# A hybrid transformer layer on one core: scale and shift in two halves of the features, with the first key/value products between them

## The chip, the core and the metric

The kernel runs on one core of a Trainium2 chip. The metric is the device time of one launch in microseconds (us). Engines are called by their names: TensorE (PE in the profile, with PEld for its weight loads), VectorE (DVE), ScalarE (ACT), GpSimd (POOL) and SyncE (SP), which issues most of the loads.

## What is computed

One layer of a diffusion backbone over 1024 latent tokens and 256 context tokens of 1024 features: attention and a gated MLP side by side, then a mixture of 16 experts that choose their tokens. The part that matters here is the start, cut from the reference:

```python
sh1, sc1, gt1, sh2, sc2, gt2 = split(silu(c) @ w_mod + b_mod, 6)      # also for c_ctx
h = rmsnorm(x, g_mix) * (1 + sc1) + sh1                               # modulate
k, v = split(h @ w_kv, 2)                                             # keys_values
```

All of it is needed at float32 precision. TensorE's fast format for 4-byte numbers (float32r in the program) keeps fewer bits, so the kernel splits an operand into a rounded high part and a remainder and adds up three products (high·high, high·low, low·high).

## The kernel before, in words

Only the first 80 us are touched. The program is one straight list per engine (`tc.manual_schedule`): every engine runs its instructions in the order in which the Python code emits them, and an engine that waits holds all that stands behind it.

**Rows of scale and shift.** The first 2048 columns of `w_mod` (1024 of shift, 1024 of scale) are loaded as eight blocks n = 0 to 7 of 512 features by 512 columns, 1 MB each (`mod_load`, L238). Two blocks make one column block of 512. `CB` (L236) sets the order: first both halves of scale, then both of shift. For each block `mod_rows(n)` (L241) splits the weights (`split_to`, L146: ScalarE rounds, L147, VectorE subtracts, L148) and TensorE multiplies them with the four columns `c4` (high and low part of silu(c) and of silu(c_ctx)): eight products of 4 x 512 (L255, L256). `mod_columns` (L258) copies the 4 x 512 result out of PSUM (VectorE, L260) and turns it into columns with four small products (L262). When all four column blocks are there, L296 adds the bias and L297 forms the gain `G1`.

**Tokens.** `x_prep` (L160) takes 128 tokens at a time: a sum of squares on ScalarE (L165), a small step on VectorE (L84), a power on GpSimd (L85), and a scaling on VectorE (L168). The square writes a one-column scratch `r` of which there are three.

**Modulation and first products.** `kv_group(g, side, steps)` (L198) does keys and values of four token tiles (g = 0 and 1) or two (g = 2, the context) over the eight feature blocks j of 128. `modulate(g, n, j)` (L182) transposes block j of the tiles on TensorE (L187), applies scale and shift on ScalarE (L191, `h`), rounds it on VectorE (L193) and forms the remainder on VectorE or, for j = 2, 4, 6 of group 0 (`LOW_P`), on GpSimd (L195). It runs two blocks ahead of the products (L219 to L221, twelve of 128 x 256 per block). `side` is other work that is put between the blocks, `steps[j]` pieces of it after block j: in group 0 `x_prep` of token tiles 4 to 7, in groups 1 and 2 that of the context and the splitting of the next weights (ScalarE and GpSimd). The last two blocks of group 0 already modulate the first two blocks of group 1, so these need token tiles 4 to 7 scaled.

**Loads.** SyncE issues in program order; a load into a buffer in use waits at the head of its queue. The key/value weights (2 x 0.5 MB, L286) go into `rkv`, the buffer of block n = 2.

Of the kernel before, what the change touches and what calls it, by code (L numbers as in the profile page):

```python
# [8 lines left out]
F32 = mybir.dt.float32  # L9
# [4 lines left out]
OP = mybir.AluOpType  # L14
# [3 lines left out]
P = 128  # L18
# [6 lines left out]
DJ = D // P  # L25
# [22 lines left out]
def layer(ctx: ExitStack, tc: tile.TileContext, a, out, dbg=None):  # L48
    nc = tc.nc
# [8 lines left out]
    consts = pool("consts")  # L58
# [29 lines left out]
    NV = 32 + 48 + 8 + 8  # L88
    colv = consts.tile([P, NV], F32, name="colv")
    csil = consts.tile([P, DJ, 2], F32, name="csil")  # L90
    c4 = consts.tile([P, DJ, 4], F32R, name="c4")
    modc = consts.tile([P, 16, 2], F32, name="modc")
    modl = consts.tile([P, 32], F32, name="modl")
    B1, B2 = modc[:, 0:8, :], modl[:, 8:16]
    G1 = consts.tile([P, DJ, 2], F32, name="G1")
# [34 lines left out]
    psA = pool("psA", 1, space=PSUM)  # L130
# [4 lines left out]
    vecs = xs.tile([NV, P], F32, name="vecs")  # L135
# [3 lines left out]
    pv = psA.tile([P, 512], F32, name="tp", bufs=3)  # L139
    nc.tensor.transpose(pv[:, :16], vecs[:16], ident[:16, :16])  # L140
    nc.scalar.activation(csil.rearrange("p j i -> p i j"), pv[:, :16].rearrange("p (i j) -> p i j", i=2), AF.Silu)

    nc.vector.tensor_copy(c4[:, :, 0:2], csil)
    nc.vector.tensor_sub(c4[:, :, 2:4], csil, c4[:, :, 0:2].bitcast(F32))

    def split_to(hi, lo, src, eng=None):  # L146
        nc.scalar.copy(hi, src)  # L147
        (eng or nc.vector).tensor_tensor(lo, src, hi.bitcast(F32), op=OP.subtract)  # L148

    XS = {}  # L150
    gm4 = gm_tiles(F32)

    def x_load(kt):

        XS[kt] = gm4[kt // 2 - 2][:, kt % 2 * D:(kt % 2 + 1) * D] if 4 <= kt < 8 else xs.tile(
            [P, D], F32, name="x", bufs=4)
        nc.sync.dma_start(XS[kt], a["x"][kt * P:(kt + 1) * P, :] if kt < NT else
                          a["ctx"][(kt - NT) * P:(kt - NT + 1) * P, :])
# [23 lines left out]
    def modulate(g, n, j):  # L182

        i = 1 if g == 2 else 0
        pt = psA.tile([P, 512], F32, name="tp", bufs=3)[:, :n * P]
        for t in range(n):
            nc.tensor.transpose(pt[:, t * P:(t + 1) * P], XS[g * 4 + t][:, j * P:(j + 1) * P], ident)  # L187
        h = xs.tile([P, 512], F32, name="h", bufs=2)[:, :n * P]
        pv, hv = (w.rearrange("p (t c) -> p t c", t=n) for w in (pt, h))
        parts = [(slice(0, 2), HA[0]), (slice(2, 4), HA[1])] if g == 0 else [(slice(0, n), HH1 if g == 1 else HHC[0])]  # L190
        nc.scalar.activation(h, pt, AF.Identity, scale=G1[:, j, i:i + 1], bias=B1[:, j, i:i + 1])  # L191
        for t, hi in parts:
            nc.vector.tensor_copy(hi[:, :, j, :], hv[:, t])  # L193
        for t, hi in parts:
            (nc.gpsimd if j in LOW_P[g] else nc.vector).tensor_tensor(HL[g][:, t, j, :], hv[:, t], hi[:, :, j, :].bitcast(F32),  # L195
                                                                      op=OP.subtract)

    def kv_group(g, side, steps):  # L198

        n = 2 if g == 2 else 4  # L200
        ps = [psA.tile([P, 512], F32, name="pj", bufs=4) for _ in range(n)]
        if g == 0:
            modulate(g, n, 0)
            modulate(g, n, 1)
            split_to(*wkv2, rkv[:, 2:4, :])
        for j in range(DJ):
            if j + 2 < DJ:
                modulate(g, n, j + 2)
            elif g < 2:

                if g == 1 and j + 2 == DJ:
                    gmc = [w.rearrange("p (t j c) -> p t j c", t=2, j=DJ) for w in gm_tiles(F32R)]
                    HHC.append(gmc[0])
                    HL.append(gmc[1])
                modulate(g + 1, 4 if g == 0 else 2, j + 2 - DJ)
            for t in range(n):
                hh = (HHC[0][:, t] if g == 2 else h_part(0, g * 4 + t))[:, j, :]
                hl = HL[g][:, t, j, :]
                nc.tensor.matmul(ps[t][:, :256], hh, wkv[j // 4][0][:, j % 4, :], start=(j == 0), stop=False)  # L219
                nc.tensor.matmul(ps[t][:, :256], hh, wkv[j // 4][1][:, j % 4, :], start=False, stop=False)  # L220
                nc.tensor.matmul(ps[t][:, :256], hl, wkv[j // 4][0][:, j % 4, :], start=False, stop=(j == DJ - 1))  # L221
# [9 lines left out]
    wraw = [rawp.tile([P, 4, 512], F32, name="raw") for _ in range(2)]  # L231
# [1 line left out]
        w = w.rearrange("p t j c -> p (t j c)").rearrange("p (n a b) -> p n a b", n=2, a=4)  # L233
        wraw += [w[:, 0], w[:, 1]]
    wraw += [rawp.tile([P, 4, 512], F32, name="raw") for _ in range(2)]
    CB = (2, 3, 0, 1)  # L236

    def mod_load(n):  # L238
        nc.sync.dma_start(wraw[n], rows(a["w_mod"], n % 2 * 512, 512, CB[n // 2] * 512, 512))

    def mod_rows(n):  # L241
        jh = n % 2
        if jh == 0:
            XS["pr"] = psA.tile([P, 512], F32, name="pj", bufs=4)
        pr = XS["pr"]
        pair = w_pair()
        if n < 7:
            for h in range(2):
                split_to(*pair[h], wraw[n][:, h * 2:h * 2 + 2, :])
        for jj in range(4):  # L250
            j = jh * 4 + jj
            wh, wl = w_part(pair, jj)
            if n == 7:
                split_to(wh, wl, wraw[n][:, jj, :])
            nc.tensor.matmul(pr[:4, :], c4[:, j, :], wh, start=(j == 0), stop=False)  # L255
# [12 lines left out]
    for n in range(2, 8):  # L268
        mod_load(n)
    for kt in range(4):  # L270
        x_load(kt)
    pr = None
    for n in range(8):
        mod_rows(n)
        if n == 2:
            pv = psA.tile([P, 512], F32, name="tp", bufs=3)
            nc.tensor.transpose(pv[:, :NV], vecs, ident[:NV, :NV])
            nc.vector.tensor_copy(colv, pv[:, :NV])
            gmixc, gffnc, bmodc, bsc, gfc = (colv[:, i:j] for i, j in ((16, 24), (24, 32), (32, 80), (80, 88), (88, 96)))
        if n % 2 == 0 and n:  # L280
            mod_columns(n // 2 - 1, pr)
        pr = XS["pr"]
        if n == 3:
            rkv = wraw[2]
            for h in range(2):
                nc.sync.dma_start(rkv[:, h * 2:h * 2 + 2, :].rearrange("p a b -> p (a b)").rearrange(  # L286
                    "p (j c) -> p j c", j=4), rows(a["w_in"], h * 512, 512, 512, 256))
            for kt in range(4, 8):
                x_load(kt)
    wkv = w_pair()  # L290
    xst = x_steps(range(4))
    next(xst)
    mod_columns(3, pr)
    for _ in range(2):
        next(xst)
    nc.vector.tensor_tensor(modc, pm1, bmodc[:, :16].unsqueeze(2).to_broadcast([P, 16, 2]), op=OP.add)  # L296
    nc.vector.scalar_tensor_tensor(G1, modc[:, 8:16, :], 1.0, gmixc.unsqueeze(2).to_broadcast([P, DJ, 2]),  # L297
                                   op0=OP.add, op1=OP.mult)
    for _ in xst:
        pass  # L300
    split_to(*wkv[0], rkv[:, 0:2, :])
# [25 lines left out]
    hl1, HH1 = h1_tiles(F32R)  # L327
    HL.append(hl1)
    HHC = []
    kv_group(0, x_steps(range(4, 8)), (1, 1, 2, 2, 2, 1, 1, 1))  # L330
    ws = chain(x_steps((8, 9)), w_steps())
    kv_group(1, ws, (1,) * 8)
    kv_group(2, ws, (1,) * 8)
# [70 lines left out]
    n = 0  # L404
# [1211 lines left out]
```

## Time and profile before

| what | before |
|---|---|
| time, median of 3 runs | 1779.95 us (1779.63 to 1780.12) |
| profiled execution | 1780.84 us, span 1779.1 us |
| TensorE busy | 1708.8 us, 96% of the span |
| VectorE / ScalarE / GpSimd busy | 1591.9 / 1244.1 / 519.9 us |
| the chain that ended last | TensorE 79%, VectorE 14% |

The profile is of one execution. A busy share is an average over very different stages; for a change in one stage the timeline and the chain of waits of that stage are read. TensorE's instructions overlap, so the chain, which gives start-to-start distances, is the better source for the cost of a product than its recorded duration.

### The profile page before, as it was taken

What the parts mean: (1) busy time and instruction counts of PE and PEld (TensorE: products, weight loads), DVE (VectorE), ACT (ScalarE), POOL (GpSimd) and SP (SyncE); (2) the same over time, 40 slices, a digit from 0 to 9 for tenths busy, and PEclk for the clock granted to TensorE, in tenths of its full rate; (3) what the DMA queues carried; (4) which work ended last, traced back from release to release, by engine and by line L of the source; (5) the groups of instructions that cost most, each with busy time, mean ns of one, the idle gap of its engine ahead of it and who ended that gap; (6) DMA issues with size and microseconds to landing.
All of it is one profiled execution on the core that took longest, in us unless ns stands there. A gap on an engine that the chain in (4) does not pass through costs nothing.

```text
span 1779.1 us, 24500 instructions
## 1 busy us (share of the span) xinstructions
PE 1708.8 (96%) x8586; PEld 1405.4 (79%) x8586; DVE 1591.9 (89%) x2371; ACT 1244.1 (70%) x1663; POOL 519.9 (29%) x358
## 2 busy tenths in 40 slices
PE   7999999999999969999999999999999999999997
PEld 4888878778788858777778888888888888888885
DVE  7778777999858999999999999999999999999997
ACT  6632356666653348777777887888878878878886
POOL 1433467787851112423331101101101101101013
PEclk9999999999999979999999999999999999999999
DMA  9357200000025678999999999999999999999994
GB/s 355 102 155 233 84 1 1 18 8 24 13 96 202 236 263 315 346 363 365 360 359 374 392 385 378 390 384 375 389 383 380 386 384 380 385 386 385 378 325 185
DMA packets 204971, 485.69 MB, mean 273 GB/s; under 512 B 10448, under 2 KB 12848, under 8 KB 204848
## 3 DMA queue, kind: packets, MB, share of 16 engines
q1 hardware_dynamic: 200096, 466.83, 70.8%
q0 software_dynamic: 4752, 17.30, 3.8%
q8 instruction: 67, 1.10, 0.3%
q14 instruction: 56, 0.46, 0.1%
HBM read 463.13 MB, written 20.97 MB: 272 GB/s over the span
## 4 chain that ended last, share of the span: by engine, by line
PE 79%; DVE 14%; issue 3%; ACT 2%; DMA 1%; POOL 1%; SPq 0%; POOLq 0%; DVEq 0%; ACTq 0%
PE p L1533 24%; PE p L1536 12%; PE py L1523 6%; PE py L1522 6%; PE py L1524 6%; DVE wlo L148 3%; PE po L768 3%; PE pj L691 2%; PE pj L693 2%; PE pj L692 2%; DVE mx L654 2%; PE tp L1322 2%; DVE ph L753 2%; PE pj L958 2%; PE pj L960 1%
## 5 line engine op out<-in xcount | busy, mean ns | idle before, releaser
L148 DVE TENSOR_TENSOR wlo<-raw,whi 128x1024 fp32r<-128x1024 f32 (+1 forms) x556 | 661.6, 1231 | 46.8 <-ACT whi L147 42.9
L147 ACT CAST whi<-raw 128x1024 fp32r<-128x1024 f32 (+1 forms) x590 | 593.1, 1021 | 118.8 <-PE p L1536 67.1
L755 POOL TENSOR_TENSOR pl<-pf,ph 128x512 fp32r<-128x512 f32 x160 | 218.1, 1385 | 52.3 <-DVE ph L753 19.6
L1533 PE MATMUL p<-whi,xb 128*128 128x512 f32 x512 | 204.9, 400 | 0.0
L1533 PE MATMUL p<-whi,xa 128*128 128x512 f32 x512 | 204.6, 400 | 0.0
L1533 PE MATMUL p<-wlo,xa 128*128 128x512 f32 x512 | 200.0, 391 | 0.3 <-DVE wlo L148 0.2
L1533 PE MATMUL p<-wlo,xb 128*128 128x512 f32 x512 | 199.8, 390 | 0.0
L1523 PE MATMUL py<-wlo,thl 128*128 128x512 f32 x504 | 198.5, 394 | 0.0
L1522 PE MATMUL py<-whi,thl 128*128 128x512 f32 x504 | 197.6, 392 | 0.0
L1524 PE MATMUL py<-whi,thl 128*128 128x512 f32 x504 | 196.3, 389 | 0.0
L1536 PE MATMUL p<-whi,xb 128*128 128x512 f32 x512 | 158.1, 390 | 0.4 <-DVE xb L1485 0.4
L1536 PE MATMUL p<-whi,xa 128*128 128x512 f32 x512 | 158.1, 390 | 0.0
L748 ACT ACTIVATE pf<-st 128x512 f32<-128x512 f32 x160 | 94.9, 598 | 70.3 <-PE st L746 61.4
L148 DVE TENSOR_TENSOR wlo<-H,whi 128x1024 fp32r<-128x1024 f32 x106 | 131.6, 1265 | 9.4 <-ACT whi L147 8.3
L148 DVE TENSOR_TENSOR wlo<-gm,whi 128x1024 fp32r<-128x1024 f32 (+1 forms) x111 | 133.0, 1218 | 6.6 <-ACT whi L147 6.1
L147 ACT CAST whi<-H 128x1024 fp32r<-128x1024 f32 x110 | 115.9, 1055 | 24.1 <-PE p L1536 18.5
L147 ACT CAST whi<-gm 128x1024 fp32r<-128x1024 f32 (+1 forms) x111 | 114.7, 1046 | 15.7 <-PE py L1524 8.4
L1340 POOL DMA_INDIRECT acc<-ye,idx x15 | 38.1, 2539 | 291.7 <-DVE ye L1337 283.6
L1536 PEld LDWEIGHTS p<-whi,xb 128*128 128x128 f32 x512 | 96.0, 188 | 21.5 <-DVE xb L1485 0.8
L1536 PEld LDWEIGHTS p<-whi,xa 128*128 128x128 f32 x512 | 96.1, 188 | 20.8
L1533 PEld LDWEIGHTS p<-wlo,xa 128*128 128x128 f32 x512 | 96.3, 188 | 19.6 <-DVE wlo L148 1.1
L1522 PEld LDWEIGHTS py<-whi,thl 128*128 128x128 f32 x504 | 94.6, 188 | 21.6
(376 smaller groups left out, 3677.1 us busy)
## 6 DMA issues: line engine op xcount, KB each, us to landing
raw<-in_w_dram SPq DMA_DIRECT2D x271, 1024.0 KB, 8.0
H<-in_w_dram SPq DMA_DIRECT2D x55, 1024.0 KB, 8.3
gm<-in_w_dram SPq DMA_DIRECT2D x54, 1024.0 KB, 8.3
raw<-in_w_mod_dram SPq DMA_DIRECT2D x64, 256.0 KB, 3.4
raw<-in_w_mod_dram SPq DMA_DIRECT2D x4, 1024.0 KB, 7.4
raw<-in_w_in_dram SPq DMA_DIRECT2D x16, 256.0 KB, 3.6
raw<-in_w_out_dram SPq DMA_DIRECT2D x4, 1024.0 KB, 5.0
xr<-in_x_dram SPq DMA_DIRECT2D x8, 512.0 KB, 6.0
```

Source lines behind the costliest of these rows:

```text
L147: nc.scalar.copy(hi, src)
L148: (eng or nc.vector).tensor_tensor(lo, src, hi.bitcast(F32), op=OP.subtract)
L654: U["mx"] = nc.vector.tensor_reduce(out=mx[:, h, pp:pp + 1], in_=pa_, axis=AX.X, op=OP.max)
L748: nc.scalar.activation(pf, pst, AF.Exp, scale=HD ** -0.5)
L755: (nc.vector if kt in PL_DVE else nc.gpsimd).tensor_tensor(pl, pf, ph.bitcast(F32), op=OP.subtract)
L768: nc.tensor.matmul(po[:, sl], st[:, blk], mv[:, sl], start=(k == 0 and o == 0 and n == 0), stop=(k == NK - 1 and n == 2), skip_group_check ...
L1340: nc.gpsimd.indirect_dma_start(out=acc, out_offset=bass.IndirectOffsetOnAxis(ap=idx[:, e:e + 1], axis=0), in_=G["ye"], in_offset=None, com ...
L1522: nc.tensor.matmul(PY[e][cb], th, hi[:, sl], start=fst, stop=False)
L1523: nc.tensor.matmul(PY[e][cb], th, lo[:, sl], start=False, stop=False)
L1524: nc.tensor.matmul(PY[e][cb], tl, hi[:, sl], start=False, stop=lst)
L1533: nc.tensor.matmul(p, xh[:, j, :], w[:, jj, :], start=(j == 0 and w is pr[0]), stop=False)
L1536: nc.tensor.matmul(p, xl[:, j, :], pr[0][:, jj, :], start=False, stop=(j == DJ - 1))
```

## The change

The two halves of the features (0 to 511 and 512 to 1023) get their scale and shift apart. `CB` becomes (2, 0, 3, 1): blocks n = 0 to 3 are scale and shift of the first half, n = 4 to 7 those of the second. `mod_done(h)` forms bias and gain of one half. The first half is done ahead of `kv_group(0)`; the row products of the second half are called from inside it, as `behind`: after feature block 0 `mod_rows(4)`, after 1 `mod_rows(5)`, after 2 `mod_rows(6)`, after 3 `mod_rows(7)` with both `mod_columns`, `mod_done(1)` and the split of the second key/value weights. The modulation of blocks 4 and 5 comes after that, and the steps of token tiles 4 to 7 come three each after blocks 3, 4 and 5.

Of each pair of blocks the first (even n) is no longer split: TensorE multiplies the loaded float32 weights with `cfull`, a float32 copy of silu(c) in four columns (two of them zero): four products instead of eight. The second (odd n) is split as before, 512 columns at a time.

In PSUM two token tiles of a group share a bank, so that a group needs two banks and the two running row results have the other two. The loads are issued in the new order: blocks 0 to 3, token tiles 0 to 3, first key/value weights, blocks 4 to 7, second key/value weights, token tiles 4 to 7.

```diff
-    def kv_group(g, side, steps):
+    def kv_group(g, side, steps, behind=()):
...
-        ps = [psA.tile([P, 512], F32, name="pj", bufs=4) for _ in range(n)]
+        banks = [psA.tile([P, 512], F32, name="pj", bufs=4) for _ in range(n // 2)]
+        ps = [banks[t // 2][:, t % 2 * 256:(t % 2 + 1) * 256] for t in range(n)]
         if g == 0:
             modulate(g, n, 0)
             modulate(g, n, 1)
-            split_to(*wkv2, rkv[:, 2:4, :])
         for j in range(DJ):
             if j + 2 < DJ:
-                modulate(g, n, j + 2)
+                if g or j not in (2, 3):
+                    modulate(g, n, j + 2)
...
+            if j < len(behind):
+                behind[j]()
+            if g == 0 and j == 3:
+                modulate(g, n, 4)
+                modulate(g, n, 5)
             for _ in range(steps[j]):
                 next(side, None)
...
-    CB = (2, 3, 0, 1)
+    CB = (2, 0, 3, 1)
...
-        pair = w_pair()
-        if n < 7:
-            for h in range(2):
-                split_to(*pair[h], wraw[n][:, h * 2:h * 2 + 2, :])
+        if jh:
+            pair = w_pair()
         for jj in range(4):
             j = jh * 4 + jj
+            if jh == 0:
+                nc.tensor.matmul(pr[:4, :], cfull[:, j, :], wmr[n][:, jj, :], start=(j == 0), stop=False)
+                continue
             wh, wl = w_part(pair, jj)
-            if n == 7:
-                split_to(wh, wl, wraw[n][:, jj, :])
+            split_to(wh, wl, wmr[n][:, jj, :])
...
+    mod_rows(0)
+    mod_rows(1)
...
+    mod_rows(2)
+    mod_columns(0, XS["pr", 0])
+    rkv = wraw[2]
...
+    rkv_load(0)
+    for n in range(4, 8):
+        mod_load(n)
+    rkv_load(1)
+    for kt in range(4, 8):
+        x_load(kt)
+    mod_rows(3)
...
+    def mod_rest():
+        mod_rows(7)
+        mod_columns(2, XS["pr", 2])
+        mod_columns(3, XS["pr", 3])
+        mod_done(1)
+        split_to(*wkv2, rkv[:, 2:4, :])
+
+    kv_group(0, x_steps(range(4, 8)), (0, 0, 0, 3, 3, 3, 0, 0),
+             (lambda: mod_rows(4), lambda: mod_rows(5), lambda: mod_rows(6), mod_rest))
-    kv_group(0, x_steps(range(4, 8)), (1, 1, 2, 2, 2, 1, 1, 1))
```

Three places show how the instructions move. In the names `tp` is a transpose's result, `pj` and `pk` are results in PSUM, `H` and `HL` the high and low part of the modulated tokens, `cfull` and `c` the conditioning columns; `HL_133`, `HL_136`, `HH_137` and `raw` stand for load buffers.

TensorE in `kv_group(0)`, from the last product of feature block 0 on. Before:

```order
L221 MATMUL pj<-whi,HL_110 128x256
L187 MATMUL tp<-ident,x 128x128 x4
L219 MATMUL pj<-whi,H_94 128x256
L220 MATMUL pj<-wlo,H_94 128x256
L221 MATMUL pj<-whi,HL_110 128x256
```

With the change:

```order
L225 MATMUL pj<-whi,HL_111 128x256
L264 MATMUL pj<-HH_137,cfull 4x512 x4
L190 MATMUL tp<-ident,x 128x128 x4
L225 MATMUL pj<-whi,H_95 128x256
L225 MATMUL pj<-wlo,H_95 128x256
```

Four row products in full float32 stand between block 0 and the transposes ahead of block 1.

ScalarE from the squares of token tiles 0 to 3 to the last `h` of group 0. Before:

```order
L165 ACTIVATE jk,r<-x 128x1024 x4
L147 CAST whi<-HL_133 128x1024
L191 ACTIVATE h<-tp,modc,G_83 128x512 x2
L147 CAST whi<-HL_133 128x1024
L191 ACTIVATE h<-tp,modc,G_83 128x512
L165 ACTIVATE jk,r<-gm_128 128x1024 x2
L191 ACTIVATE h<-tp,modc,G_83 128x512 x2
L165 ACTIVATE jk,r<-gm_129 128x1024
L191 ACTIVATE h<-tp,modc,G_83 128x512
L165 ACTIVATE jk,r<-gm_129 128x1024
L191 ACTIVATE h<-tp,modc,G_83 128x512 x4
```

With the change:

```order
L168 ACTIVATE jk,r<-x 128x1024 x4
L150 CAST whi<-HL_136 128x1024
L194 ACTIVATE h<-tp,modc,G_84 128x512 x4
L150 CAST whi<-HH_137 128x512 x4
L150 CAST whi<-raw 128x512 x4
L150 CAST whi<-HL_136 128x1024
L194 ACTIVATE h<-tp,modc,G_84 128x512 x2
L168 ACTIVATE jk,r<-gm_131 128x1024 x2
L168 ACTIVATE jk,r<-gm_132 128x1024
L194 ACTIVATE h<-tp,modc,G_84 128x512
L168 ACTIVATE jk,r<-gm_132 128x1024
L194 ACTIVATE h<-tp,modc,G_84 128x512 x3
```

The squares of token tiles 4 to 7 (`gm`) stood behind the third, fifth and sixth `h`; now they stand behind the sixth and seventh, and the casts of two row blocks stand behind the fourth.

SyncE, from block n = 2 on. Before:

```order
L239 DMA HL_133<-in_w_mod_dram 128x4x512 x2
L239 DMA HH_134<-in_w_mod_dram 128x4x512 x2
L239 DMA raw<-in_w_mod_dram 128x4x512 x2
L157 DMA x<-in_x_dram 128x1024 x4
L286 DMA HL_133<-in_w_in_dram 128x4x256 x2
L157 DMA gm_128<-in_x_dram 128x1024 x2
```

With the change:

```order
L251 DMA HL_136<-in_w_mod_dram 128x4x512 x2
L160 DMA x<-in_x_dram 128x1024 x4
L306 DMA HL_136<-in_w_in_dram 128x4x256
L251 DMA HH_137<-in_w_mod_dram 128x4x512 x2
L251 DMA raw<-in_w_mod_dram 128x4x512 x2
L306 DMA HL_136<-in_w_in_dram 128x4x256
L160 DMA gm_131<-in_x_dram 128x1024 x2
```

The token tiles and the first key/value weights come ahead of four blocks of `w_mod`; the key/value load waits until TensorE has read block n = 2, and the four blocks stand behind it.

## Rows read from the trace of the kernel before

**Rows 1.** The page, parts 1 and 4: busy time, and the chain by engine

```profile
PE 1708.8 (96%) x8586; PEld 1405.4 (79%) x8586; DVE 1591.9 (89%) x2371; ACT 1244.1 (70%) x1663; POOL 519.9 (29%) x358
...
PE 79%; DVE 14%; issue 3%; ACT 2%; DMA 1%; POOL 1%; SPq 0%; POOLq 0%; DVEq 0%; ACTq 0%
```

**Rows 2.** Windows: start:end, length, busy us of each engine (instructions), PEclk, DMA share

```profile
38.10:54.40 16.30, 16.30 (x128) 16.30 (x127) 13.75 (x37) 12.08 (x23) 7.67 (x10) 0.90 0.64 228
54.40:69.00 14.60, 14.60 (x126) 14.53 (x124) 11.24 (x19) 10.72 (x24) 6.30 (x6) 1.00 0.05 12
69.00:80.50 11.50, 8.44 (x62) 7.29 (x61) 10.04 (x15) 6.50 (x19) 6.43 (x5) 1.00 0.04 10
```

**Rows 3.** Timeline of ScalarE, 0 to 60 us: start, duration, line, shapes [idle before]

```profile
6.68 1.99 ACT L147 CAST whi<-raw 128x1024 fp32r<-128x1024 f32 x2 [3.45 <-DMA raw<-in_w_mod_dram]
9.50 1.99 ACT L147 CAST whi<-raw 128x1024 fp32r<-128x1024 f32 x2 [0.83 <-DMA raw<-in_w_mod_dram]
...
15.35 2.00 ACT L147 CAST whi<-HL 128x1024 fp32r<-128x1024 f32 x2 [0.80 <-DMA HL<-in_w_mod_dram]
...
26.18 2.18 ACT L147 CAST whi<-raw 128x512 fp32r<-128x512 f32 x4 [0.71 <-DMA raw<-in_w_mod_dram]
28.27 1.05 ACT L165 ACTIVATE jk<-x 128x1024 bf16<-128x1024 f32 x1
...
29.45 1.06 ACT L165 ACTIVATE jk<-x 128x1024 bf16<-128x1024 f32 x1
```

**Rows 4.** Chain, 8 to 16 us: start us, us to the next piece, what

```profile
9.63 0.43 PE pj L255
...
14.76 0.23 PE pj L256
```

**Rows 5.** Chain, 96 to 104 us, in the stage behind

```profile
98.59 0.89 PE tp L501 x8
99.48 0.23 PE pj L691
...
102.45 0.78 PE pk L397 x8
```

**Rows 6.** Chain, 26 to 56 us

```profile
28.46 0.98 PE pk L262 x8
...
31.42 0.69 DVE h L260
...
34.52 0.93 POOL r L85
35.47 0.77 DVE x L168
36.28 2.18 PE tp L187 x9
...
52.54 0.44 PE tp L187 x4
...
54.42 0.44 PE tp L187 x4
```

**Rows 7.** Groups by line and form, 0 to 82 us: count, busy us, mean ns

```profile
L191 ACT ACTIVATE h<-tp,modc,G 128x512 f32<-128x512 f32 x16 | 12.4, 781 | 8.9 <-PE tp L187 8.1 <-ACT whi L147 0.6
...
L195 POOL TENSOR_TENSOR HL<-h,H 128x256 fp32r<-128x256 f32 x6 | 5.2, 885 | 7.2 <-DVE H L193 7.2
...
L193 DVE CAST H<-h 128x256 fp32r<-128x256 f32 x16 | 4.9, 349 | 0.8 <-ACT h L191 0.8
...
L148 DVE TENSOR_TENSOR wlo<-raw,whi 128x512 fp32r<-128x512 f32 x4 | 2.5, 672 | 0.0
```

**Rows 8.** Windows of 1 us about the change of the clock

```profile
34.00:35.00 1.00, 0.33 (x1) 0.14 (x1) 1.00 (x3) 0.93 (x1) 0.48 (x1) 0.82 0.98 385
35.00:36.00 1.00, 0.48 (x1) 0.18 (x1) 0.56 (x2) 0.00 (x0) 0.43 (x1) 0.50 1.02 406
...
41.00:42.00 1.00, 1.00 (x9) 1.00 (x8) 0.45 (x3) 0.92 (x2) 0.74 (x2) 0.77 1.05 389
```

More of the change, by code (lines that the diff above doesn't have):

```diff
@@ L91, in layer @@
     c4 = consts.tile([P, DJ, 4], F32R, name="c4")
+    cfull = consts.tile([P, DJ, 4], F32, name="cfull")
     modc = consts.tile([P, 16, 2], F32, name="modc")
@@ L141, in layer @@
     nc.scalar.activation(csil.rearrange("p j i -> p i j"), pv[:, :16].rearrange("p (i j) -> p i j", i=2), AF.Silu)
+    nc.vector.memset(cfull, 0.0)
+    nc.vector.tensor_copy(cfull[:, :, 0:2], csil)
     nc.vector.tensor_copy(c4[:, :, 0:2], csil)
@@ L218, in kv_group @@
                 hl = HL[g][:, t, j, :]
-                nc.tensor.matmul(ps[t][:, :256], hh, wkv[j // 4][0][:, j % 4, :], start=(j == 0), stop=False)
-                nc.tensor.matmul(ps[t][:, :256], hh, wkv[j // 4][1][:, j % 4, :], start=False, stop=False)
-                nc.tensor.matmul(ps[t][:, :256], hl, wkv[j // 4][0][:, j % 4, :], start=False, stop=(j == DJ - 1))
+                for k, (h, w) in enumerate(((hh, 0), (hh, 1), (hl, 0))):
+                    nc.tensor.matmul(ps[t], h, wkv[j // 4][w][:, j % 4, :], start=(j == 0 and t % 2 == 0 and k == 0),
+                                     stop=(j == DJ - 1 and k == 2), skip_group_check=True)
+            if j < len(behind):
[3 more added lines that the diff above has]
+                modulate(g, n, 5)
             for _ in range(steps[j]):
@@ L235, in layer @@
     wraw += [rawp.tile([P, 4, 512], F32, name="raw") for _ in range(2)]
-    CB = (2, 3, 0, 1)
+    wmr = wraw
+    CB = (2, 0, 3, 1)
     def mod_load(n):
-        nc.sync.dma_start(wraw[n], rows(a["w_mod"], n % 2 * 512, 512, CB[n // 2] * 512, 512))
+        nc.sync.dma_start(wmr[n], rows(a["w_mod"], n % 2 * 512, 512, CB[n // 2] * 512, 512))
     def mod_rows(n):
@@ L243, in mod_rows @@
         if jh == 0:
-            XS["pr"] = psA.tile([P, 512], F32, name="pj", bufs=4)
-        pr = XS["pr"]
-        pair = w_pair()
-        if n < 7:
-            for h in range(2):
-                split_to(*pair[h], wraw[n][:, h * 2:h * 2 + 2, :])
+            XS["pr", n // 2] = psA.tile([P, 512], F32, name="pj", bufs=4)
+        pr = XS["pr", n // 2]
+        if jh:
+            pair = w_pair()
         for jj in range(4):
             j = jh * 4 + jj
+            if jh == 0:
+                nc.tensor.matmul(pr[:4, :], cfull[:, j, :], wmr[n][:, jj, :], start=(j == 0), stop=False)
+                continue
             wh, wl = w_part(pair, jj)
-            if n == 7:
-                split_to(wh, wl, wraw[n][:, jj, :])
-            nc.tensor.matmul(pr[:4, :], c4[:, j, :], wh, start=(j == 0), stop=False)
+            split_to(wh, wl, wmr[n][:, jj, :])
+            nc.tensor.matmul(pr[:4, :], c4[:, j, :], wh, start=False, stop=False)
             nc.tensor.matmul(pr[:4, :], c4[:, j, :], wl, start=False, stop=(j == DJ - 1))
@@ L267, in layer @@
         nc.sync.dma_start(vecs[r0:r0 + nr], a[src].rearrange("(r p) -> r p", p=P))
-    for n in range(2, 8):
+    for n in range(2, 4):
         mod_load(n)
@@ L271, in layer, with mod_done, rkv_load @@
         x_load(kt)
[L272 to L289, printed above, removed]
+    def mod_done(h):
+        for c in (h * 4, 8 + h * 4):
+            nc.vector.tensor_tensor(modc[:, c:c + 4, :], pm1[:, c:c + 4, :],
+                                    bmodc[:, c:c + 4].unsqueeze(2).to_broadcast([P, 4, 2]), op=OP.add)
+        hs = slice(h * 4, h * 4 + 4)
+        nc.vector.scalar_tensor_tensor(G1[:, hs], modc[:, 8 + h * 4:12 + h * 4, :], 1.0,
+                                       gmixc[:, hs].unsqueeze(2).to_broadcast([P, 4, 2]), op0=OP.add, op1=OP.mult)
+    mod_rows(0)
+    mod_rows(1)
+    pv = psA.tile([P, 512], F32, name="tp", bufs=3)
+    nc.tensor.transpose(pv[:, :NV], vecs, ident[:NV, :NV])
+    nc.vector.tensor_copy(colv, pv[:, :NV])
+    gmixc, gffnc, bmodc, bsc, gfc = (colv[:, i:j] for i, j in ((16, 24), (24, 32), (32, 80), (80, 88), (88, 96)))
+    mod_rows(2)
+    mod_columns(0, XS["pr", 0])
+    rkv = wraw[2]
+    def rkv_load(h):
+        nc.sync.dma_start(rkv[:, h * 2:h * 2 + 2, :].rearrange("p a b -> p (a b)").rearrange(
+            "p (j c) -> p j c", j=4), rows(a["w_in"], h * 512, 512, 512, 256))
+    rkv_load(0)
[5 more added lines that the diff above has]
+    mod_rows(3)
     wkv = w_pair()
@@ L292, in layer @@
     next(xst)
-    mod_columns(3, pr)
+    mod_columns(1, XS["pr", 1])
     for _ in range(2):
         next(xst)
-    nc.vector.tensor_tensor(modc, pm1, bmodc[:, :16].unsqueeze(2).to_broadcast([P, 16, 2]), op=OP.add)
-    nc.vector.scalar_tensor_tensor(G1, modc[:, 8:16, :], 1.0, gmixc.unsqueeze(2).to_broadcast([P, DJ, 2]),
-                                   op0=OP.add, op1=OP.mult)
+    mod_done(0)
     for _ in xst:
```

## The prediction

> **What bounds the kernel now.** The page comes first: TensorE is busy for 96% of the span and makes up 79% of the chain that ended last, VectorE 14% [rows 1]. So whatever lengthens or shortens TensorE's list in the touched stage should show in the time, unless TensorE stands idle there anyway. The windows answer that by stage: from 38.1 to 54.4 us (group 0) and on to 69.0 (group 1) TensorE is busy without a break; from 69.0 to 80.5 it works 8.4 of 11.5 us and waits for VectorE [rows 2]. Ahead of that loads set the pace: ScalarE starts on each 1 MB block of `w_mod` when it lands, from 6.68 us to 26.18, 2.8 us per block, so a 0.5 MB token tile takes 1.4 [rows 3]. Behind the last block comes a chain of small steps: VectorE's copy of the last row result at 31.42, columns, squares and powers, the last scaling at 35.47 + 0.77 = 36.24, and then the transposes [rows 6]. Group 0 ends with the transposes at 54.42, which are group 1's [rows 6].
>
> The change starts group 0 earlier and puts work into it. What counts is when those transposes behind group 0 come: nothing later is altered that sets the pace, so I take the shift there as the shift of the end.
>
> **The price of a full float32 row product.** The trace has no such product of 512 columns. The nearest is that of L501, 128 x 128 in full float32: four products are eight instructions in 0.89 us, 0.111 each [rows 5]. Scaled by columns, a product of 512 costs 2 x 4 x 0.111 = 0.89. But at one column (L397) an instruction still takes 0.78 / 8 = 0.098 [rows 5], so part of the 0.111 may not grow with columns. The other bound is two instructions at the distance of the rounded format, 2 x 0.23 = 0.46 [rows 5]. I take 0.89, which scales the only row of such products with more than a few columns, and keep 0.46 for the range.
>
> [...]
>
> **The front.** The first row products no longer wait for a split and start at 6.7. TensorE begins slowly: its products stand 0.43 apart at 9.63 and 0.23 at 14.76 [rows 4], so the clock rises some 5 us after the products begin to follow one another; here at about 11.8. Block 0: 5.1 us at half clock are 2.9 products of 1.78, the rest takes 1.0, end 12.8. Block 1: eight rounded products, 1.9, end 14.7; its splits are no later (landed 9.5 [rows 3], first cast 0.55, four subtractions of 0.62 [rows 7], end 12.5). Block 2: 3.6 and a small transpose, end 18.4. Columns: eight instructions in 0.98 [rows 6], end 19.4. Block 3 landed at 15.35 and is split by 18.4; products to 21.3. VectorE's copy then comes at 21.4 instead of 31.42. The small steps behind it are the same as before and took 36.24 - 31.42 = 4.8 us [rows 6], which gives 26.2 for the last scaling. The fourth token tile lands at 15.35 + 4 x 1.4 = 20.9, early enough. **Gain: 10.0 us.** The first key/value weights are issued when TensorE has read block 2, at 18.4; the queue in front of them empties only at 20.9, so I cost this wait at nothing. The eight token loads, two key/value loads and eight blocks are as many bytes as before.
>
> **What goes in.** Group 0's own products and transposes are those of before, and so is the half clock at its beginning. Added on TensorE:
> - blocks 4 and 6: 8 full products, 8 x 0.89 = **7.1**
> - blocks 5 and 7: 16 rounded products, 16 x 0.23 = **3.7**
> - two sets of columns, 2 x 0.98 = **2.0**
>
> And three holes that the orders of the engines make:
> - **Hole A, at block 5.** ScalarE's casts of block 5 stand behind `h` of feature block 3, whose transposes stand behind block 4 on TensorE. From the end of those transposes: `h` 0.78, VectorE's casts and remainders to 2.1, then four subtractions of 0.62 to 4.6, the last product to 4.9. TensorE itself has 12 products (52.54 to 54.42 less the 0.44 of four transposes [rows 6]: 1.44) and 8 x 0.23, together 3.3. **1.6.** Block 7 is split behind it by ScalarE and VectorE while TensorE does blocks 2, 6 and 3: no hole.
> - **Hole B, at feature block 4.** It needs the second half's gain, which comes 0.5 behind the last columns (three small VectorE steps); `h` ends at 1.4, but VectorE is in the key/value split until 1.75; two casts of 0.35 at most, so the first product is at 2.3, while the transposes fill 1.3. GpSimd's remainders (0.885 each [rows 7]) end at 3.2 and 4.1 and hold the third product of the first and of the third tile: 0.7 more. **1.7.**
> - **Hole C, ahead of group 1's first transposes.** These need token tile 7, whose square stands on ScalarE behind two `h`, three squares and another `h`. From the last columns: 0.55 + 2 x 0.8 + 3 x 1.18 [rows 3] + 0.8 + 1.18 = 7.7. Its power on GpSimd waits behind the remainders of block 6 (to 8.9), takes 0.93 [rows 6], and the scaling 0.77: 10.6. TensorE is through with feature block 5 at 6.4. **4.2.** Before, these squares stood between the `h` of blocks 2 to 5 and cost nothing; that cover is gone.
>
> Sum: -10.0 + 7.1 + 3.7 + 2.0 + 1.6 + 1.7 + 4.2 = **+10.3 us**. The splits of four blocks that ScalarE and VectorE no longer make were beside the loads and give nothing more than the earlier start.
>
> **The clock in hole C.** In the thin stretch between 31.4 and 36.3 the granted clock fell to half between 34 and 35 us and rose between 41 and 42, some 5 us after the transposes set in [rows 6, 8]. Hole C is about as long. If the clock falls there, some 5 us at half cost 2.5; if it stays, nothing. Nothing decides it; I take the middle, 1.2. **Total +11.5**: the profiled execution of 1780.84 would become 1792.3; the median shown is 0.9 below that execution, and 1779.95 + 11.5 = **1791.5**.
>
> **The rivals.**
> - *Cheap products.* A full product costs 0.46. Inside group 0 that saves 8 x 0.43 = 3.4. In front the token tiles then set the pace: 20.9 + 1.18 + two small steps + 0.93 + 0.77 is about 24.0, 2.2 earlier. 10.3 - 5.6 + 1.2 = +5.9, **1785.8**. For it: the one-column row. Against it: the scaled row.
> - *A late front.* The clock does not rise while the first products run. Blocks 0 to 2 then take 7.1 + 3.4 + 7.1 and end at 24.3 instead of 18.4. SyncE holds the key/value load and the four blocks behind it all that time, and the loads run dry from 20.9 on. Everything comes 5.9 later: +17.4, **1797.4**. For it: before, the first five microseconds ran at half clock. Against it: they ended then, with products no denser than these.
> - *Not slower.* A full product of 512 columns costs no more than one in the rounded format, 0.23, in the row blocks of front and group 0. Then 8 x 0.66 = 5.3 goes inside and the same 2.2 in front: +2.8, **1782.8**. It decides from about 0.33 us per product down, where the sum falls under 3.6 us. For it: such products leave ScalarE and VectorE free, and half of the splits go. Against it: full products are two instructions each, and a single one of 128 columns takes 0.111.
> - *Given back later.* In group 2 TensorE idles 3.1 us behind VectorE [rows 2]. Could a late start use that up? VectorE's steps there follow TensorE's transposes and move with them, so I expect nothing; at most the forecast falls to +8.4.
>
> That the change does something else than it says is not a case: the orders show the full products, the new places of the squares and the one load that waits for TensorE.
>
> **How the numbers follow.** A measurement of this kernel can tell 0.2%, 3.6 us, from no change. The forecast, with or without the fall of the clock and with holes a microsecond or two off (1788 to 1795), gets 0.68; cheap products 0.14; the late front 0.08; not slower 0.08, of which 0.05 within 3.6 us and 0.03 below, where holes would have to be smaller besides; 0.02 is left for something later still. Slower is 0.68 + 0.14 + 0.08 + 0.02 = 0.92. The range takes in the cheap products without a fall of the clock (+4.7, 1784.6) and reaches up to the late front: 1784.5 to 1797.5.
>
> **What would show it.** In the profile of the changed kernel: TensorE's four products of L264 in `kv_group(0)` some 3.6 us long at full clock; the first product of group 0 near 28 us instead of 38.1; VectorE's subtraction of block 5 as the releaser of L269; an idle stretch of some 4 us on TensorE ahead of the transposes from `gm`, ended by VectorE's scaling L171; group 1's transposes near 64 to 66 us instead of 54.42; all behind that alike, only later. It is wrong if L264's products stand under 0.4 us apart, if group 1 starts before 58 us, or if the stages behind 80 us change their length.

## The result, and the profile after

The changed kernel takes **1806.81 us** (median of 4 runs, 1806.42 to 1807.85), the kernel before on the same chip 1780.03. The ratio is 1.0151, 95% interval 1.0134 to 1.0169: 26.8 us slower, and above the forecast range of 1784.5 to 1797.5. The profiled execution has a span of 1805.0 us and a mean granted clock of 0.987.

The page, parts 1 and 4, against [rows 1]:

```profile
PE 1731.5 (96%) x8586; PEld 1410.2 (78%) x8586; DVE 1588.6 (88%) x2375; ACT 1236.2 (68%) x1661; POOL 515.3 (29%) x358
...
PE 80%; DVE 13%; issue 3%; ACT 2%; DMA 1%; POOL 1%; POOLq 0%; SPq 0%; ACTq 0%; DVEq 0%
```

TensorE is busy 22.7 us longer with the same number of instructions. The touched stage, in the chain of waits (start, time to the next piece, what), against [rows 4, 6]:

```profile
6.88 5.50 PE pj L264 x8
...
14.41 3.53 PE pj L264 x8
...
20.90 0.69 DVE h L273
...
24.99 0.76 DVE x L171
...
25.80 2.18 PE tp L190 x9
27.98 2.56 PE pj L225 x12
30.54 3.88 PE pj L264 x8
...
37.07 0.61 DVE wlo L151
...
37.73 0.39 PE pj L269
...
39.93 1.41 PE pj L225 x12
41.34 3.53 PE pj L264 x8
...
48.35 1.87 PE pk L275 x16
...
60.38 0.68 DVE gm L171
...
61.10 0.48 PE tp L190
61.58 2.56 PE pj L225 x12
...
66.63 0.45 PE tp L190 x4
```

The copy of the last row result needed for the first half comes at 20.90 instead of 31.42, the last scaling ends at 25.75 instead of 36.24. Four full float32 products (eight instructions) take 3.53 us at full clock, 0.88 each. Group 1's transposes that stood at 54.42 stand at 66.63: **+12.2 us**, where the forecast had +11.5. TensorE's waits between 27 and 67 us (us in total, times, longest):

```profile
PE tp L190 <- DVE gm L171: 2.1, 2, 1.3
PE tp L190 <- DVE r L84: 1.8, 1, 1.8
PE pj L269 <- DVE wlo L151: 0.9, 1, 0.9
PE pj L225 <- DVE H L196: 0.5, 1, 0.5
PE pj L225 <- POOL HL L198: 0.3, 1, 0.3
```

The starts on TensorE's timeline about holes B and C (start, duration): the twelve transposes before feature block 4, the four ahead of block 5, the first of group 1's, and the first product of block 6:

```profile
50.15 1.53 PE L190 MATMUL tp<-ident,x 128*128 128x128 f32 x12
...
54.27 0.60 PE L190 MATMUL tp<-ident,x 128*128 128x128 f32 x4
...
56.15 0.30 PE L190 MATMUL tp<-ident,gm 128*128 128x128 f32 x1
...
61.23 0.56 PE L225 MATMUL pj<-whi,H 128*128 128x256 f32 x1
```

And the clock in hole C, in windows of 1 us (columns as in [rows 8]): TensorE idles from 56.2 on but for single transposes, the clock is at half from 59 us and rises in the window from 65:

```profile
58.00:59.00 1.00, 0.33 (x1) 0.14 (x1) 1.00 (x3) 0.20 (x1) 1.00 (x2) 0.76 0.94 350
59.00:60.00 1.00, 0.47 (x1) 0.18 (x1) 1.00 (x5) 0.00 (x0) 0.75 (x1) 0.50 0.82 243
...
65.00:66.00 1.00, 1.00 (x9) 1.00 (x9) 0.12 (x1) 0.82 (x2) 0.00 (x0) 0.82 0.00 0
```

So the touched stage came out nearly as worked out, and the other half of the loss lies elsewhere. The stages by the starts of their products, from the timelines of both (us):

| | before | after | later by |
|---|---|---|---|
| group 1's transposes ([rows 6]) | 54.42 | 66.63 | 12.2 |
| first product of the next stage (L691, now L723) | 80.5 | 94.0 | 13.5 |
| first product of the experts (L1533, now L1565) | 651.57 | 667.08 | 15.5 |
| last product of the experts | 1759.55 | 1785.45 | 25.9 |

The expert stage, whose code the change does not touch, has grown from 1108.0 to 1118.4 us: 10.4. The granted clock is 1.00 in both there. Its products, grouped by line and form (busy us, mean ns of one | idle time before), before from 660 to 1740 us:

```profile
L1533 PE MATMUL p<-whi,xa 128*128 128x512 f32 x496 | 198.3, 400 | 0.0
...
L1533 PE MATMUL p<-wlo,xa 128*128 128x512 f32 x496 | 193.6, 390 | 0.0
...
L1536 PE MATMUL p<-whi,xa 128*128 128x512 f32 x496 | 153.1, 390 | 0.0
```

and after, from 680 to 1760 us:

```profile
L1565 PE MATMUL p<-whi,xa 128*128 128x512 f32 x494 | 199.7, 404 | 0.0
...
L1565 PE MATMUL p<-wlo,xa 128*128 128x512 f32 x494 | 194.6, 394 | 0.0
...
L1568 PE MATMUL p<-whi,xa 128*128 128x512 f32 x494 | 155.1, 395 | 0.0
```

Nobody waits there. Each product of w1 and w3 (stationary operand `xa` or `xb`, moving operand `whi` or `wlo`) is 4 to 5 ns longer; there are about 3000. The products of w2 (stationary `thl`) are not: their three lines have means of 392, 394 and 389 ns before (L1522 to L1524) and of 393, 390 and 392 now. From start to start, where one such product follows another, w1 and w3 stand 227.9 ns apart before and 232.6 after, w2 229.0 and 229.1 (means over the starts in the traces).

What differs for these instructions is where their operands lie. `cfull`, 8 x 4 numbers, is 128 bytes per partition in the pool of constants, which the program allocates first on the left side of the memory. All left-side tiles behind it, `xa`, `xb` and the H tiles among them, moved up by 128 bytes. The right side, with `whi`, `wlo` and `thl`, stayed. Before, `xa`, `xb` and the weights all lay at 224 modulo 256 bytes; now `xa` and `xb` lie at 96. Another difference is the order in which the buffers of the split weights are used, since the change splits four blocks fewer. These are the two theories: **addresses** or **buffers** (with everything that merely comes later).

### The profile page after: what moved, and what is told of

It reads as the page before. It is cut to its first block, busy times and chain, and to the rows that moved or that the text cites. A ratio compares the mean times of both kernels' runs of the same rounds, so it can differ in the third digit from the quotient of the medians.

```text
span 1805.0 us, 24482 instructions
## 1 busy us (share of the span) xinstructions
PE 1731.5 (96%) x8586; PEld 1410.2 (78%) x8586; DVE 1588.6 (88%) x2375; ACT 1236.2 (68%) x1661; POOL 515.3 (29%) x358
## 4 chain that ended last, share of the span: by engine, by line
PE 80%; DVE 13%; issue 3%; ACT 2%; DMA 1%; POOL 1%; POOLq 0%; SPq 0%; ACTq 0%; DVEq 0%
PE p L1565 25%; PE p L1568 12%; PE py L1554 6%; PE py L1556 6%; PE py L1555 6%; PE po L800 3%; DVE wlo L151 2%; PE pj L723 2%; PE pj L725 2%; PE pj L724 2%; DVE mx L686 2%; PE tp L1354 2%; DVE ph L785 2%; PE pj L990 1%; PE pj L992 1%
## 5 line engine op out<-in xcount | busy, mean ns | idle before, releaser
L1565 PE MATMUL p<-whi,xb 128*128 128x512 f32 x512 | 207.1, 404 | 0.0
L1565 PE MATMUL p<-whi,xa 128*128 128x512 f32 x512 | 206.9, 404 | 0.0
L1565 PE MATMUL p<-wlo,xa 128*128 128x512 f32 x512 | 201.9, 394 | 0.2 <-DVE wlo L151 0.2
L1565 PE MATMUL p<-wlo,xb 128*128 128x512 f32 x512 | 201.7, 394 | 0.0
L1568 PE MATMUL p<-whi,xb 128*128 128x512 f32 x512 | 160.8, 395 | 0.4 <-DVE xb L1517 0.4
L1568 PE MATMUL p<-whi,xa 128*128 128x512 f32 x512 | 160.7, 395 | 0.0
L1568 PEld LDWEIGHTS p<-whi,xb 128*128 128x128 f32 x512 | 96.3, 188 | 23.4 <-DVE xb L1517 0.8
L1568 PEld LDWEIGHTS p<-whi,xa 128*128 128x128 f32 x512 | 96.4, 188 | 22.7
L1565 PEld LDWEIGHTS p<-wlo,xa 128*128 128x128 f32 x512 | 96.6, 189 | 20.9 <-DVE wlo L151 1.1
L1565 PEld LDWEIGHTS p<-whi,xb 128*128 128x128 f32 x512 | 96.5, 188 | 20.6 <-ACT xb L1507 0.2
```

Source lines behind the costliest of these rows:

```text
L1565: nc.tensor.matmul(p, xh[:, j, :], w[:, jj, :], start=(j == 0 and w is pr[0]), stop=False)
L1568: nc.tensor.matmul(p, xl[:, j, :], pr[0][:, jj, :], start=False, stop=(j == DJ - 1))
```

## The experiments

### Addresses alone, and the change without them

**e1_before_pad128** is the kernel before with the tile and nothing else, **e6_before_pad256** the same with 256 bytes, **e2_after_home** the changed kernel with `cfull` in the memory of a tile that is first written later.

```diff
# e1; in e6 the tile is [P, DJ, 8]
     c4 = consts.tile([P, DJ, 4], F32R, name="c4")
+    cfull = consts.tile([P, DJ, 4], F32, name="cfull")
# e2, from the changed kernel
-    cfull = consts.tile([P, DJ, 4], F32, name="cfull")
     modl = consts.tile([P, 32], F32, name="modl")
+    cfull = modl.rearrange("p (j c) -> p j c", c=4)
```

> The kernel before with one more tile of 128 bytes per partition behind c4, which nothing writes or reads: every left-side tile behind it, the experts' inputs xa and xb among them, lies 128 bytes further on, as in the changed kernel; the order of the work is that of before. Theory 1 (addresses): the +10.4 us that the changed kernel loses in the expert stage and the some +2 in the attention come from this shift, so 1780 becomes 1790 to 1794, with the expert stage (first to last product of w1/w3 and w2 there) about 1132 us where before has 1122. Theory 2 (another rotation of the split weights' buffers, or the later start of all that follows): the shift costs nothing, 1779 to 1781 and 1122 us.

> The changed kernel with cfull kept in the memory of modl, which is first written much later: no tile is added, and all left-side tiles lie where they lay before the change. The order of the work is the changed one. Theory 1 (addresses): 1806.8 - 10.4 - 2 = about 1794 (1793 to 1797), the forecast's own sum. Theory 2 (rotation of the buffers, later start): 1805 to 1808.

> As e1_before_pad128 with a tile of 256 bytes. If theory 1 holds and what matters is the place within 256 bytes, this is 1780 again; if any shift from the old place costs, about 1790; if the cost depends on the place in a longer stretch, anything between or beyond, a gain too. By theory 2 it is 1779 to 1781.

Measured, as ratios to the kernel before: e1 **1.0071** (1.0054 to 1.0088; 1793.27 us), e2 **1.0072** (1.0055 to 1.0089; 1793.59), e6 **1.0005** (0.9995 to 1.0014; 1781.82). An unused tile of 128 bytes costs the kernel before some 13 us, taking it out of the changed kernel gives back as much, and twice the bytes cost nothing that can be told. The expert stage is 1118.4 us long in e1 and 1108.0 in e2 and e6. The group of e1, 660 to 1740 us, and that of e2, 680 to 1760 us:

```profile
L1534 PE MATMUL p<-whi,xa 128*128 128x512 f32 x484 | 195.8, 404 | 0.0
```

```profile
L1565 PE MATMUL p<-whi,xa 128*128 128x512 f32 x504 | 201.6, 400 | 0.0
```

e2 keeps the changed order of the buffers and its later start, and has the old durations; so buffers and lateness are out. It is the addresses.

### Which place counts

**m1_phases** is no layer: 256 groups of 16 rounded products of 512 columns, with the stationary and the moving operand at all multiples of 32 bytes within 512.

```diff
+    for s in range(16):
+        for m in range(16):
...
+                so, mo = SO + 8 * s + 128 * (k % 8), MO + 8 * m + 512 * (k % 4)
+                nc.tensor.matmul(p, st[:, so:so + 128], mv[:, mo:mo + 512], start=(k == 0), stop=(k == 15))
```

> A measurement by itself: all of the layer is left out, and TensorE runs 256 groups of 16 rounded 512-column products back to back, nothing else on the chip. The stationary blocks (512 bytes per partition apart) begin 0, 32, ... 480 bytes behind a multiple of 512, and for each of these the moving pieces (2048 bytes apart) too. Theory 1a (it is the place of the stationary or of the moving operand, or of both against each other, that costs inside TensorE's own reading): the groups differ, about .228 us a product where both lie at 224 modulo 256, about .233 where the stationary one lies at 96, and a pattern shows which of the two places counts. Theory 1b (the place only counts against what other engines and the DMA read and write at the same time): all 256 groups take the same time.

The timeline of TensorE, one row per group (start, duration). The stationary operand is at 0, the moving one at 32, 64 and so on to 256:

```profile
19.51 3.90 PE L76 MATMUL pb<-mv,st 128*128 128x512 f32 x16
23.25 3.83 PE L76 MATMUL pa<-mv,st 128*128 128x512 f32 x16
26.92 3.89 PE L76 MATMUL pb<-mv,st 128*128 128x512 f32 x16
30.65 3.89 PE L76 MATMUL pa<-mv,st 128*128 128x512 f32 x16
...
45.57 3.79 PE L76 MATMUL pa<-mv,st 128*128 128x512 f32 x16
49.20 1.10 PE L76 MATMUL pb<-mv,st 128*128 128x512 f32 x4
```

The time of a group is the distance to the next start: 3.74 at 32, 3.67 at 64, 3.73 at 96 and again at 128, 3.63 at 256, that is .2337, .2294, .2331 and .2269 us a product. With the stationary operand at 96 the short group is the one in which the moving one is at 96 too (first row: 208.93 - 205.28 = 3.65), and 64 bytes further on comes 216.33 - 212.66 = 3.67:

```profile
205.28 3.81 PE L76 MATMUL pb<-mv,st 128*128 128x512 f32 x16
208.93 3.90 PE L76 MATMUL pa<-mv,st 128*128 128x512 f32 x16
212.66 3.83 PE L76 MATMUL pb<-mv,st 128*128 128x512 f32 x16
216.33 3.89 PE L76 MATMUL pa<-mv,st 128*128 128x512 f32 x16
```

The pattern follows the difference of the two places modulo 256, in all 16 positions of the stationary operand: from the starts of the products 227.0 to 228.2 ns each at difference 0, 228.6 to 230.0 at 64, and 232.2 to 234.1 at the other six. Besides filling the operands and writing out zeros the program has these products alone, and in m2_fine, which begins alike, VectorE and GpSimd are busy for 0.00 us from 20 to 40 us, at a DMA share of 0.00 and a granted clock of 1.00. Only the places of the two operands change from group to group, so the difference of 3.63 and 3.74 us needs no other engine and no transfer. How it arises no run shows. The kernel before has difference 0 for w1 and w3 and 64 for w2, the changed one 128 and 64.

**e13_before_both_shifted** asks the same in the layer: e1 with the weights moved too.

```diff
# from e1
     whl = pool("whl", 6, side="right")
+    gap = rawp.tile([P, 32], F32, name="gap", bufs=1)
```

> As e1_before_pad128, with another unused tile of 128 bytes on the right side ahead of the weights: xa, xb and the H tiles lie at 96 modulo 256 as in e1_before_pad128, and whi and wlo move down from 224 to 96 too. If it is the place of one operand against the other that costs, as in the bare groups of m1_phases, the loss is gone: 1779 to 1782, w1/w3 products' mean durations 400 and 390. Rival (the place of the stationary tiles by itself costs in the layer): 1791 to 1794, 404 and 394 as in e1_before_pad128.

Measured: ratio **0.9989** (0.998 to 0.9999; 1779.73 us). The loss is gone though `xa` and `xb` lie where they lay in e1, and the group reads as before:

```profile
L1535 PE MATMUL p<-whi,xa 128*128 128x512 f32 x496 | 198.3, 400 | 0.0
```

**m2_fine** goes through the differences in steps of 4 bytes, with other strides and formats (same program, other groups).

> As m1_phases, all of the layer left out; groups of 32 rounded products with the moving operand d bytes behind the stationary one modulo 256, d from -64 to 64 in steps of 4, then with one of the operands or both kept at one place, with each stationary block used twice in a row, products of 256 columns with d from 0 to 224, and full float32 products with d of 0, 32, 64 and 128. From m1_phases: .2269 us a product at d = 0, .2337 at 32, .2294 at 64, .2331 at 128. Theory A (place of one operand against the other within 256 bytes, in steps of 32): all d between two multiples of 32 cost alike, d = 0 is the least, and the blocks' strides change nothing. Theory B (finer steps count): some d of less than 32 gives less than .2269. Full float32 products, by the forecast's 0.89 at full clock: .88 to .89 at d = 128 (there in the changed kernel), and at d = 0 either the same or less by up to four times .0062.

From the starts of the products in its trace, ns a product: 227.0 at 0, 226.7 at -16, 229.2 at 64, and between 229 and 240 almost everywhere else (239.9 at -12, 237.2 at 4). So finer steps do count, but none beats 0 by more than 0.3 ns, and there is nothing to gain beyond the old place. The blocks' strides hardly matter (227.0 to 228.2 at 0, 232.2 at 128). Full float32 products are two instructions of 429 ns each, 0.858 us together, at each of the four differences run (0, 32, 64 and 128).

**e8_before_th_aligned** moves `thl` to difference 0 in the kernel before, by an unused tile.

```diff
     rt = pool("rt", side="right")
+    gap = rt.tile([P, 48], F32, name="gap")
```

> The kernel before with an unused tile of 192 bytes ahead of the experts' middle activations (thl, the stationary operand of all w2 products): they lie at 224 modulo 256 then, as the weights whi and wlo do, instead of at 160. If the place of the stationary against the moving operand modulo 256 sets a product's time, each of the 1512 w2 products falls from .2294 towards .2269 us, up to 3.8 us in all, and as in e1_before_pad128 (12.8 of 3960 x .0062 = 24.6 us) about half of it is seen: 1776 to 1779, w2 products' mean duration about 390 each. Rival (only xa and xb count, or the w2 products are held by something else): 1780.

The w2 products' distance falls from 229.0 to 226.8 ns and the expert stage from 1108.0 to 1105.9 us, but the time only to 1778.97: ratio 0.9994 (0.9985 to 1.0003), which cannot be told from no change.

### The terms of the touched stage

**e5_squares_early** is aimed at hole C: e2 with the squares and scalings of tokens 512 to 1023 behind the casts of block 7.

```diff
     def mod_rest():
         mod_rows(7)
+        split_to(*wkv2, rkv[:, 2:4, :])
+        for _ in range(8):
+            next(side, None)
         mod_columns(2, XS["pr", 2])
...
-        split_to(*wkv2, rkv[:, 2:4, :])
```

> As e2_after_home, and the squares and scalings of tokens 512-1023 stand right behind the casts of block 7, where ScalarE has nothing to do for 10 us, instead of behind the last columns. If the hole ahead of group 1's first transposes is made by these scalings (as forecast: 4.2 us, and the clock's fall in it 1.2), the time is 4 to 6 us below e2_after_home and group 1's transposes start 4 to 5 us earlier. Rival: the hole passes to the next thing that is late there (the activations of feature blocks 6 and 7, or the landing of the tokens), and less than 1 us is won.

Ratio 1.0047 (1.0031 to 1.0064; 1790.04 us) against 1.0072 for e2: 3.6 us less, a little under what was expected. In the traces group 1's first product comes 4.9 us earlier (62.5 against 67.4) and the last product of the experts 4.1. TensorE's waits for token tiles 4 to 7 are gone: the hole was where the forecast said. The clock's part of it was not saved: in e5 the granted clock stood at half from 52 to 58 us, while TensorE was busy.

**e9_late_blocks_split** rounds and splits the row blocks 4 and 6 again, in e5; **e10_late_split_order** also puts the scalings behind feature blocks 3 and 4 (two each) and gives `r` four buffers.

```diff
# e9, from e5
-        if jh:
+        full = n in (0, 2)
+        if not full:
             pair = w_pair()
# e10, from e9: in mod_rest the squares only (the rest is left out)
-        for _ in range(8):
-            next(side, None)
+        for g in gx:
+            next(g)
```

> As e5_squares_early, but the row blocks 4 and 6, whose full float32 products lie between the key/value products, are rounded and split like the others; blocks 0 and 2 stay in full float32. By the forecast's prices the eight full products there (8 x 0.88 = 7.0 us) become 16 rounded ones (16 x .23 = 3.7): 3 to 3.5 us less than e5_squares_early, so 1786 to 1787, if ScalarE's casts (4 x .53 us a block) and the buffers of the split weights keep up. Rival: the casts or the buffers come late and make holes like hole A (0.9 us in the changed kernel) ahead of blocks 4 and 6: 1788 to 1791.

> As e9_late_blocks_split, but only the squares of tokens 512-1023 stand behind the casts; their scalings stand behind feature blocks 4 and 5, so that the copy of the last columns doesn't queue behind them on VectorE (in e9_late_blocks_split TensorE waited 4.7 us for that copy). Theory (full float32 products are dear, as in the forecast's sum): with that hole gone the saving of 3 to 3.5 us on the eight late products is seen, and the time is 1786 to 1788, 2 to 4 us below e5_squares_early. Rival (they stand where TensorE would have waited for casts or buffers anyway): 1789 to 1791, as e5_squares_early and e9_late_blocks_split.

Ratios 1.0065 (1.0049 to 1.008) and 1.0061 (1.0046 to 1.0077): both misses, no gain over e5. In e9 the copy of the last columns queues on VectorE, as its row of TensorE's waits (28 to 62 us) shows:

```profile
PE pk L276 <- DVE h L274: 4.7, 1, 4.7
```

In e10 2.4 us of that wait are left, and waits of 1.3 us for the scalings come in. VectorE now subtracts for four blocks in a stretch where it also makes the modulated tokens. Up to its last row product e9 is ahead of e5 by 2.8 us (it starts at 44.98 against 47.77), near the 3 to 3.5 of the forecast's prices; then comes the wait of 4.7, and the granted clock stands at half from 48 to 58 us. So the price of the full products shows ahead of the wait, and not in the time of these two.

**e11_before_full_even** asks it in the front: the kernel before, only its even blocks in full float32 (`cfull` in `modl`). **e12_before_full_even_aligned** is that with e8's tile.

```diff
# e11, in mod_rows of the kernel before
+            if jh == 0:
+                nc.tensor.matmul(pr[:4, :], cfull[:, j, :], wraw[n][:, jj, :], start=(j == 0), stop=False)
+                continue
```

> The kernel before, with one part of the change alone: the even row blocks by full float32 products (cfull in the memory of modl, no address moved), all eight blocks still ahead of the tokens. By the forecast's prices TensorE works 16 x 0.88 - 32 x .23 = 6.7 us more there; the blocks land every 2.7 us and TensorE waited between them, so that most of it should be covered. If the front is set by the landings and the chain behind the last block: 1778 to 1781, first key/value product 36.5 to 38.5. Rival (the front becomes TensorE's): first key/value product and the end 2 to 5 us later.

> e11_before_full_even and the 192 bytes of e8_before_th_aligned together, as a candidate that beats both kernels: e8_before_th_aligned gave 1779.0 against 1780.0. If the two gains add: 1776 to 1779. Rival: 1779 to 1781, no difference from before.

e11: ratio 1.0027 (1.0016 to 1.0038; 1785.63 us); the first key/value product comes at 43.45 instead of 38.11, 5.3 later, and TensorE is busy from 6.82 on almost without a break. The rival came true, a little beyond its 2 to 5 us: TensorE becomes the front's bound. Part of the 5.3 is the granted clock, which stood at half from 22 to 25 us here and at 1.00 before: an estimated 1.7 us, half of the 3.4 us that windows of 1 us show at half. Two of its four blocks, in its timeline, the first as slow as the first products of [rows 4], the other at full speed:

```profile
6.82 5.88 PE L257 MATMUL pj<-raw,modl 128*4 128x512 f32 x8 [3.88 <-DMA raw<-in_w_mod_dram]
...
14.58 3.60 PE L257 MATMUL pj<-HL,modl 128*4 128x512 f32 x8
```

e12: 1.0015 (1.0006 to 1.0024; 1783.4 us), not better than before; that it is better than e11 the intervals do not show. No version that was run clearly beats the kernel before: the lowest ratio is e13's 0.9989, whose interval ends at 0.9999.

## Why the prediction was wrong, and where it was right

**The step that failed** is the sentence "nothing later is altered that sets the pace, so I take the shift there as the shift of the end", and with it "all behind that alike, only later". The change alters the place of the operands of some 4000 later products. With `cfull` kept out of the allocation (e2) the time is 1793.59, ratio 1.0072, where 1791.5 had been forecast for the whole change. The other 13 us are the tile of 128 bytes: 10.4 in the expert stage and the rest ahead of it, where the other 512-column products with split weights went from 229.0 to 232.1 ns, some 860 times, 2.7 us. The bare groups would give more, 3072 x .0062 = 19 us in the expert stage. In the layer the products lost 4.7 ns instead of 6.2, which makes 14.4, and only 10.4 of these reach the length of the stage. Why the layer loses less than the bare groups is not settled.

The prediction did name the sign that it would be wrong by, "if the stages behind 80 us change their length", and no rival had that mechanism: all four were about group 0 to 2.

**The steps that held.** Forecast against measured, in us:

| step | forecast | measured |
|---|---|---|
| front, last scaling at | 26.2 | 25.75 |
| a full product at full clock | 0.89 | 0.88 |
| blocks 4 and 6 | 7.1 | 3.88 + 3.53 = 7.4 |
| two sets of columns | 2.0 | 1.87 |
| block 5 with hole A | 1.84 + 1.6 = 3.4 | 36.44 to 39.77 = 3.3 |
| block 7 | 1.84 | 46.33 to 48.28 = 1.9 |
| hole B | 1.7 | 50.15 to 54.27 = 4.12, less 2.76: 1.4 |
| hole C | 4.2 | 56.15 to 61.23 = 5.08, less 0.44: 4.6 |
| clock in hole C | 1.2 | about 1.8 |
| group 1's transposes | +11.5 | +12.2 |

Holes B and C are read from start to start on TensorE's timeline, less what the same work takes without a hole: 0.44 us for four transposes and 1.44 for twelve products, by [rows 6] (2.76 is three times the one and once the other). The idle times listed for them, 0.8 and 3.9 us, are shorter, because a product's record lasts longer than its place in the stream (0.28 us, at a distance of 0.12). The clock's price is 2.56 against 1.41 us for a block of twelve products, 0.85 against 0.45 for four transposes and 1.64 against 1.41 for the last block.

With the front's 10.5 these steps make -10.5 + 7.4 + 1.9 + 3.3 + 1.9 + 1.4 + 4.6 + 1.8 = +11.8 of the 12.2. No term is off by more than 0.6. The clock's 1.2 was the middle of two cases, 2.5 and nothing, so its nearness is no merit: the clock fell, and for the first 2 us of that TensorE was idle but for two transposes. The slow beginning of the front is read from distances alone: rounded products stand 0.43 us apart and later 0.23 [rows 4], and with the change the first four full products take 5.50 us and the next four 3.53. The granted clock is given as 1.00 there (before from 6 to 15 us, after from 6 to 16), so half a clock in those microseconds is the author's estimate.

The rivals of cheap products and "not slower" fell by L264's 3.53 us, that of the late front by the last scaling at 25.75. A full product takes 0.88 us in place (3.53 for four) and 0.858 back to back in m2_fine, a little under the 0.89 of the forecast.

"Given back later" was wrong in the other direction: from group 1 to the next stage 1.3 us were lost. In group 2 TensorE works only about 6 of 9 us ([rows 2] and the windows here; 5.9 from 69 to 78 us before). In the kernel before the granted clock held through it at 1.00, and in e1, with the same order and almost the same busy times, it fell behind it, to 0.52 from 78 to 81 us. Windows of 3 us, before:

```profile
75.00:78.00 3.00, 1.64 (x12) 1.20 (x11) 2.93 (x4) 1.25 (x3) 1.98 (x2) 1.00 0.00 0
78.00:81.00 3.00, 3.00 (x25) 2.88 (x24) 1.49 (x5) 1.31 (x6) 0.00 (x0) 1.00 0.36 96
```

and e1:

```profile
75.00:78.00 3.00, 1.65 (x9) 1.20 (x10) 2.93 (x4) 1.22 (x3) 2.33 (x2) 1.00 0.00 0
78.00:81.00 3.00, 3.00 (x16) 3.00 (x16) 1.84 (x5) 0.98 (x2) 0.00 (x0) 0.52 0.13 26
```

The changed kernel's profile shows the same fall (0.56 from 90 to 93 us). It fell in e2, e5, e6 and e10 to e13 too, and not in e8 and e9, in one profiled execution of each. So this microsecond or so belongs to no part of the change for certain; what decides it was not tried.

## What to carry to other kernels

A new tile moves every tile that is allocated behind it on its side; here an unused one of 128 bytes cost some 13 us (e1) and one of 256 nothing that can be told (e6). After such a change compare the addresses of the operands of the products that make up the time, and keep the stationary and the moving operand of rounded 512-column products at the same place modulo 256 bytes, where they took .2269 us in m1_phases against .2331 at 128 apart (reuse an existing tile, or fill up to 256). When a stage that a change does not touch grows evenly, with nobody waiting, look at the mean duration by line before looking for a wait. Full float32 products save splits on the other engines and cost TensorE about 0.88 us against 0.46 for two rounded ones, so they can pay only where TensorE would have waited; in e11, where it was busy almost without a break, the ratio to the kernel before was 1.0027.

## What the runs showed of the hardware

- A rounded 512-column product took from .2267 to .2399 us back to back, by the difference of its operands' places modulo 256 bytes: .2270 to .2282 at 0, .2286 to .2300 at 64 and .2322 to .2341 at the other multiples of 32 (m1_phases). Steps under 32 bytes count as well: .2267 at -16, .2399 at -12, .2372 at 4 (m2_fine).
- Full float32 products did not feel it (429.0 to 429.2 ns per instruction at 0, 32, 64 and 128, m2_fine), and products of 256 columns felt it differently: 119.4 ns at 0, 114.0 at 192, from the same trace. The first key/value products might gain by that; it was not tried.
- The granted clock held in one execution and fell in another in the same thin stretch of one program order, group 2: from 78 to 81 us it was 1.00 before and 0.52 in e1.
